# Retention heads: TensorE's order written out in the program instead of chosen by the scheduler, and a new order of the first head's loads

## The chip, the cores and the metric

The kernel runs on one core of one Trainium2 chip, as one program. The time is the device time of one execution in microseconds. A core has five engines that each work through a list of instructions in order: TensorE (PE in the profile; its weight loads are listed apart as PEld), VectorE (DVE), ScalarE (ACT), GpSimd (POOL) and SyncE (SP), which issues most of the DMAs. An instruction that needs another engine's result waits on a semaphore, and all that stands behind it in its list waits with it. Matmuls write to PSUM, in banks of 128 x 512 floats; VectorE and ScalarE take the results from there.

## The reference

Two layers of a decoder: a gated short convolution, then retention; behind each a SwiGLU feed-forward part (width 2816), RMS norms between. The width is 1024, with 512 prompt tokens and 32 sample tokens (8 sequences of 4), so 544 tokens. Retention has 4 heads with keys of 256 and values of 512. Cut to the part that the change touches:

```python
def retention_chunkwise(q, k, v, s0):              # chunks of 128 tokens
    def step(S, qkv):
        qc, kc, vc = qkv
        scores = jnp.einsum('bhid,bhjd->bhij', qc, kc) * decay
        inner = jnp.einsum('bhij,bhjv->bhiv', scores, vc)
        cross = jnp.einsum('bhid,bhdv->bhiv', qc, S) * cross_w[:, :, None]
        S_new = S * chunk_decay[:, None, None] + jnp.einsum('bhjd,bhjv->bhdv', kc * state_w[:, :, None], vc)
        return S_new, inner + cross
    ...
def retention_mixer(x, s0, pos, w_in, gn_g, w_out):
    z = x @ w_in
    q, k, v, g = jnp.split(z, [QK_DIM, 2 * QK_DIM, 2 * QK_DIM + V_DIM], axis=-1)
    ...
    q = rotary(q, pos)
    k = rotary(k, pos) * (HEAD_DK ** -0.5)
    o, S = retention_chunkwise(q, k, v, s0)
    ...                                             # each head's o: minus its mean, over its deviation
    out = (jax.nn.silu(g) * of) @ w_out
    return out, S
```

The sample sequences bring states of their own (8 x 4 heads x 256 x 512 floats, 16.8 MB), which are read, used and written back updated. Outputs are the tokens after the last norm, the convolution's buffers and the retention states.

## The kernel before

**Number format.** All products are of float32 precision by three products of rounded parts: each operand is split into a rounded part `h` (ACT, line 188) and a rest `l` (DVE, line 189); `mm3` (lines 163 to 165) and `project` (line 175) issue `h*h`, `h*l` and `l*h`. Every weight tile of 512 KB is thus loaded by SP, copied by ACT and subtracted by DVE before TensorE can use it (`load_piece`). With `adding=True` the subtraction is left to a DMA of GpSimd's queue that adds while it writes (line 196).

**Stages.** Convolution to about 159 us, the first feed-forward part to 575, then retention, and from 1083 on the second feed-forward part. The retention's part ahead of the heads stands in `ahead`: k, q and v of head 0 (to 631), then as jobs the gates of heads 0 to 2. The results go to memory and are loaded again (`qk_made`, `v_made`, `gate_made`). The four heads follow, in a loop (line 1299 on), at about 695, 812, 914 and 1016 us.

**A head.** While head h's sample operands are made, TensorE computes v of head h+1 in `value_products`: 8 k tiles, each 4 token tiles by 3 products of 128x512 (lines 816 to 818), and twice 4 small products for the sample tokens (line 824). The weights of v come in four pieces of two k tiles. Between them stand small steps: `keys` (transposes of the rotated keys, whose split parts are `knh` and `knl`), `sample_scores` (line 1211, result `s2`), `value_sample` (`v2`), `sample_operands` (`vs`, `kns`). Then:

- `state(c)`, for two halves of the prompt: 12 products into two banks (lines 163 to 165). After the first half the bank is split into `mid` (ACT, DVE), and the second half goes on in the same bank.
- `sample_outputs(i)` and `states_update(i)`, for four quarters of the sample states: four products with the state S (line 1237), four outer products (line 1253), and two updates `S = gamma * S + product` by DVE (line 1258, 128x1024 each); S is loaded in 1 MB and stored again. Three buffers hold S.
- `scores(c)`: 12 products of 128x256, masked by DVE into `sf` and split into `sh` and `sl`.
- `inner(i)`, for four token tiles: products with `mid` and of `sh`, `sl` with v. `normalized` takes mean and deviation with DVE (lines 1164, 1165, 222), GpSimd (line 223) and DVE again (line 1168, result `yn`).
- `gated_pair`, `gated`: four transposes of a `yn` (line 1192) and a product with the gate by DVE (line 1195).
- the next head's k and q: four `qk_project` of 48 products each (line 175), followed by DVE's rotation (lines 1011 to 1016).
- `out_project`: `yh` and `yl` from the gated values, 192 products by `project`.

The last head has no next v, k and q: its own gates are computed there instead (`gate_project`, four times 48 products).

**What sets the order.** The program is a list of operations in the order of the Python code; a scheduler places each on its engine by planned times, so that an engine's list can differ from the order of the code. `tc.issue_after(x)` keeps an operation behind another. Before, the heads are left to the scheduler with some such marks. Buffers are tiles with tags: two tiles of one tag share memory, and the later one waits for the last use of the earlier one. PSUM comes by `bank()` (single, `sm` in the profile) and `psum()` (a pair, `mm`).

Of the kernel before, what the change touches and what calls it, by code (L numbers as in the profile page):

```python
# [21 lines left out]
NH = 4  # L22
# [26 lines left out]
def hybrid_decode_kernel(ctx: ExitStack, tc: tile.TileContext, a: dict, o: dict):  # L49
# [211 lines left out]
    def drain(steps):  # L261
        for _ in steps:
            pass

# [532 lines left out]
    def value_products(h, xs, first=None, then=None, ws=None, sw=None):  # L797
# [3 lines left out]
        if ws is None:  # L801
            raw = []
            ws = [value_piece(h, c, raw, first is None, sw=None if c else sw) for c in range(2)]
        else:
            ws, raw = ws
        after = first() if first is not None else None
        for c in range(4):
            wh, wl = ws[c]
            if c < 2:
                ws.append(value_piece(h, c + 2, raw, first is None and c == 0, after=after if c == 0 else None))  # L810
            for k2 in range(2):
                kt = 2 * c + k2
                cw = slice(k2 * DV, (k2 + 1) * DV)
                for tt in range(4):
                    ts_, out = slice(tt * P, (tt + 1) * P), pv[tt]
                    nc.tensor.matmul(out, xh[kt][:, ts_], wh[:, cw], start=(kt == 0), stop=False)  # L816
                    nc.tensor.matmul(out, xh[kt][:, ts_], wl[:, cw], start=False, stop=False)  # L817
                    last = nc.tensor.matmul(out, xl[kt][:, ts_], wh[:, cw], start=False, stop=(kt == KT - 1))  # L818
            if c in (1, 2):
# [9 lines left out]
            if then is not None:  # L829
                then(c)  # L830
# [16 lines left out]
    def ahead(tp, fp, sw, one):  # L847
# [10 lines left out]
        qw, qpt = load_piece(a["rtqk"][0, 0], KT * P, adding=True), [bank(), bank()]  # L858
        project(qpt, *qw, 0, xh, xl, weave=steps)
# [11 lines left out]
        off(0, 0, qpt)  # L871
        xs = fp.tile([P, KT, NS], F32, tag="f", name=nm("xs"))
# [5 lines left out]
        pv, pvs = value_products(0, xs, then=operand_of, sw=sw)  # L878
# [43 lines left out]
    with ExitStack() as c2:  # L922
# [64 lines left out]
        def qk_project(h, st, which, dt, inside=None):  # L987
# [3 lines left out]
            if inside:  # L991
                project(pt, wh, wl, 0, xh, xl, last=False, ks=range(KP))
                inside()
                project(pt, wh, wl, 0, xh, xl, first=False, ks=range(KP, KT))
            else:
                project(pt, wh, wl, 0, xh, xl)
# [28 lines left out]
        def value_loaded(h, st):  # L1025
# [3 lines left out]
            nc.sync.dma_start(vw, v_made[h][:, 0:4, :])  # L1029
            st["loaded"] = nc.sync.dma_start(vsw, v_made[h][:, 4, :])  # L1030
# [9 lines left out]
        def value_sample(h, st):  # L1040

            pt = psum()
            v4 = tp.tile([P, 2, DV], F32R, tag="rot1", name=nm("v4"), bufs=1)
            split(v4[:, 0, :], v4[:, 1, :], st["v"][2])
            for i in range(2):
                nc.tensor.matmul(pt[:NS, 0, :], sum4, v4[:, i, :], start=(i == 0), stop=(i == 1))
            v2 = [tp.tile([NS, DV], F32R, tag=f"rt{i}", name=nm("v2"), bufs=1) for i in range(2)]
            split(*v2, pt[:NS, 0, :])
            st["v"][2] = v2

        def operands_made(h, st):

            qk_split(h, st, 1)
            qk_split(h, st, 0)
            sample_scores(h, st)
# [6 lines left out]
            keys(h, st)  # L1062

        def keys(h, st):
# [10 lines left out]
            split(knh, knl, pt)  # L1075
            pt = psum()
# [4 lines left out]
            st["kn"] = (knh, knl, k2)  # L1081
# [37 lines left out]
        def gate_project(h, st, n, inside=None, ws=None):  # L1119
# [3 lines left out]
            pt = [bank(), bank()] if inside else psum()  # L1123
            if inside:
                project(pt, wh, wl, 0, xh, xl, last=False, ks=range(KP))
                inside()
                project(pt, wh, wl, 0, xh, xl, first=False, ks=range(KP, KT))
            else:
                project(pt, wh, wl, 0, xh, xl)
            g = halves(st["gate"][:, n, :])  # L1130

            def scaled(p, gi, r):
                st["scaled"] = nc.vector.tensor_mul(gi, p, r)
# [25 lines left out]
        def normalized(src, tag="yn"):  # L1159
# [7 lines left out]
            yn = tp.tile([P, DV], F32, tag=tag, name=nm("yn"), bufs=2 if tag == "yn" else 1)  # L1167
# [38 lines left out]
        def sample_scores(h, st):  # L1206
# [10 lines left out]
            split(s2[:, 0, :], s2[:, 1, :], ss)  # L1217
            placed(pt[:, 1, :NS], s2[:, 0, :], s2[:, 1, :], 1)
# [42 lines left out]
        def out_project(h, st, rest=None):  # L1261
# [10 lines left out]
            split_gated(slice(0, HT if rest else T))  # L1272
            wide("mms")
            for n2 in range(4):
                wh, wl = load_piece(a["rtout"][h, n2], 2 * 4 * P)
                pts = []
                for n in range(2):
                    pts.append(psum())
                    if n2 == 0 and rest:
                        rest[n]()  # L1280
                        project(pts[n], wh, wl, n * 4 * P, yh, yl, hfs=(0,))
                    else:
                        project(pts[n], wh, wl, n * 4 * P, yh, yl)
                        residual(2 * n2 + n, pts[n])
                if n2 == 0 and rest:
                    split_gated(slice(HT, T))
                    for n in range(2):
                        project(pts[n], wh, wl, n * 4 * P, yh, yl, hfs=(1,))
                        residual(n, pts[n])
            wide("m")  # L1290

        def first_outputs(h, st):
            sample_outputs(h, st, 0)
            states_update(h, st, 0)
            states_load(h, st, 3)

        st = qk_start(0)
        qk_loaded(st)
        for h in range(NH):
            more = h + 1 < NH  # L1300
            st["S"] = {}

            def first():
                value_loaded(h, st)
                return st["loaded"] if h == 0 else None

            def then(c):
                if c == 0:
                    with tc.issue_after(last_load[0].ins) if h == 0 else ExitStack():
                        for i in range(2):  # L1310
                            states_load(h, st, i)
                elif c == 1:
                    states_load(h, st, 2)
                    operands_made(h, st)
                elif c == 2:
                    value_sample(h, st)

            if more:
                pv, pvs = value_products(h + 1, xs, first, then, None if h else next_v)
                va = tp.tile([P, 2, DV], F32, tag="rot1", name=nm("va"), bufs=1)  # L1320
                vb = [tp.tile([P, DV], F32, tag="yn", name=nm("vb")) for _ in range(2)]
                sample_operands(h, st)
# [4 lines left out]
                state(h, st, 0)  # L1327
                first_outputs(h, st)
                state(h, st, 1)
            else:  # L1330
                gw = load_piece(a["rtg"][h, 0], KT * P)
                first()
                for i in range(2):
                    states_load(h, st, i)
                gate_project(h, st, 0, lambda: operands_made(h, st), gw)
                value_sample(h, st)
                states_load(h, st, 2)
                sample_operands(h, st)
                state(h, st, 0)
                first_outputs(h, st)  # L1340
                gate_project(h, st, 1)
                state(h, st, 1)
            for c in range(2):
                scores(h, st, c)
            yn0 = normalized(inner(h, st, 0))
            sample_outputs(h, st, 1)
            yn1 = normalized(inner(h, st, 1))
            states_update(h, st, 1)
            sample_outputs(h, st, 2)
            p2 = inner(h, st, 2)  # L1350
            if more:
                nxt = qk_start(h + 1)
                for which in (1, 0):
                    qk_scale(nxt, which)
                with tc.issue_after(last_product[0].ins):
                    qk_project(h + 1, nxt, 1, 0)
                with tc.issue_after(last_product[0].ins):
                    gated_pair(h, st, (yn0, 0), (yn1, 1))
                sample_outputs(h, st, 3)
                p3 = inner(h, st, 3)  # L1360
                yn2 = normalized(p2)
                yns = normalized(st["po"])
                states_update(h, st, 2)

                def inside():
                    states_update(h, st, 3)
                    gated(h, st, yn2, 2)

                qk_project(h + 1, nxt, 1, 1, inside)
                yn3 = normalized(p3)  # L1370
                gated_pair(h, st, (yns, 4), (yn3, 3))
                qk_project(h + 1, nxt, 0, 0)
                qk_project(h + 1, nxt, 0, 1)
                out_project(h, st)
            else:
                yn2 = normalized(p2, "gt")
                gate_project(h, st, 2, lambda: states_update(h, st, 2))

                def inside():
                    sample_outputs(h, st, 3)  # L1380
                    states_update(h, st, 3)

                gate_project(h, st, 3, inside)
                with tc.issue_after(st["scaled"].ins):
                    yns = normalized(st["po"], "rot1")
                gated_pair(h, st, (yn0, 0), (yn1, 1))
                gated(h, st, yn2, 2)
                p3 = inner(h, st, 3)
                gated(h, st, yns, 4)
# [124 lines left out]
```

## Time and profile before

| | us |
|---|---|
| three runs | 1478.06, 1478.22, 1479.28 (median 1478.22) |
| profiled execution, its own time | 1478.13 |
| its span (first to last instruction) | 1475.8 |
| TensorE busy | 1458.5 (99%) |
| VectorE busy | 959.6 (65%) |
| ScalarE busy | 610.5 (41%) |
| GpSimd busy | 90.1 (6%) |
| mean granted clock of TensorE | 0.995 |

Times in the profile are in us from the span's start. A group is given as line, engine, operation, tile written <- tiles read. "Idle before" is the time that an engine stood still right before an instruction, with what released it. A group called `wh` or `w` may belong to any weight.

### The profile page before, as it was taken

To read this page: it belongs to the slowest core of one execution; us is meant where nothing else is said; L and a number is where in the kernel's file an instruction comes from. 1 tells how busy PE (TensorE), PEld (TensorE's weight loads), DVE (VectorE), ACT (ScalarE), POOL (GpSimd) and SP (SyncE) were. 2 spreads that over 40 slices of the span, in tenths; PEclk is the share of its full clock that TensorE was granted. 3 is DMA by queue.
4 is the path that set the end of the run, shared out by engine and by line. 5 is a ranking of instruction groups with operands and counts; after the bars stand their busy time and mean duration, and the time that the engine had idled before them with its cause. 6 is when DMAs were issued, how large, how long until landed. Compare 5 with 4: busy or idle time off the path is not lost.

```text
span 1475.8 us, 26100 instructions
## 1 busy us (share of the span) xinstructions
PE 1458.5 (99%) x10944; PEld 1382.9 (94%) x10944; DVE 959.6 (65%) x1470; ACT 610.5 (41%) x882; POOL 90.1 (6%) x112
## 2 busy tenths in 40 slices
PE   9999999999999999999899999999999999999998
PEld 9999999999999999799589698798799999999997
DVE  6645439847748546776686484595759857748645
ACT  5222355625425335466412322323265625525424
POOL 0100220000000003000000000000030000000002
PEclk9999999999999999999999999999999999999999
DMA  6222274232222334554784573672454232322322
GB/s 225 86 87 86 89 177 109 96 105 87 93 93 100 98 90 132 140 169 149 274 287 140 197 257 115 210 248 102 157 146 112 94 107 86 99 93 96 101 65 83
DMA packets 77445, 194.86 MB, mean 132 GB/s; under 512 B 7168, under 2 KB 24448, under 8 KB 76944
## 3 DMA queue, kind: packets, MB, share of 16 engines
q1 hardware_dynamic: 70272, 172.83, 34.6%
q0 software_dynamic: 2912, 10.56, 4.1%
q10 hardware_dynamic: 4144, 9.81, 1.7%
q8 instruction: 86, 1.41, 0.4%
q14 instruction: 31, 0.25, 0.1%
HBM read 162.29 MB, written 30.88 MB: 131 GB/s over the span
## 4 chain that ended last, share of the span: by engine, by line
PE 94%; DVE 3%; DMA 1%; issue 1%; ACT 1%; POOL 0%; DVEq 0%; POOLq 0%; ACTq 0%; SPq 0%
PE mm L175 35%; PE sm L461 30%; PE sm L175 15%; PE sm L817 2%; PE sm L818 2%; PE sm L163 2%; PE sm L816 2%; PE sm L1237 1%; PE sm L164 1%; PE sm L165 1%; DVE wl L189 1%; DMA wl<-in_rtqk_dram 1%; PE mm L1253 0%; DVE xl L201 0%; PE mm L1192 0%
## 5 line engine op out<-in xcount | busy, mean ns | idle before, releaser
L188 ACT ACTIVATE wh<-w 128x1024 fp32r<-128x1024 f32 (+4 forms) x210 | 204.5, 977 | 382.8 <-PE mm L175 185.7
L189 DVE TENSOR_TENSOR wl<-w,wh 128x1024 fp32r<-128x1024 f32 (+4 forms) x210 | 236.9, 1131 | 42.5 <-ACT wh L188 40.4
L461 PE MATMUL sm<-oh,wh 128*128 128x272 f32 x672 | 194.5, 289 | 0.0
L461 PE MATMUL sm<-oh,wl 128*128 128x272 f32 x672 | 194.2, 289 | 0.0
L461 PE MATMUL sm<-ol,wh 128*128 128x272 f32 x672 | 194.0, 289 | 0.0
L175 PE MATMUL mm<-xh,wh 128*128 128x272 f32 x804 | 170.1, 292 | 0.2
L175 PE MATMUL mm<-xh,wl 128*128 128x272 f32 x804 | 167.0, 290 | 2.4 <-DMA wl<-in_rtqk_dram 2.4
L175 PE MATMUL mm<-xl,wh 128*128 128x272 f32 x804 | 166.8, 289 | 0.0
L269 DVE TENSOR_TENSOR x<-x,mm 128x544 f32<-128x544 f32 x85 | 61.3, 721 | 144.3 <-PE mm L175 144.1
L461 PE MATMUL sm<-oh,l 128*128 128x272 f32 x504 | 145.6, 289 | 0.0
L461 PE MATMUL sm<-ol,h 128*128 128x272 f32 x504 | 145.4, 289 | 0.0
L461 PE MATMUL sm<-oh,h 128*128 128x272 f32 x504 | 145.3, 289 | 0.0
L175 PEld LDWEIGHTS mm<-xh,wl 128*128 128x128 f32 x804 | 126.1, 190 | 3.2 <-DMA wl<-in_rtqk_dram 2.6
L175 PEld LDWEIGHTS mm<-xh,wh 128*128 128x128 f32 x804 | 126.7, 190 | 1.7 <-ACT wh L188 0.5
L461 PEld LDWEIGHTS sm<-oh,wh 128*128 128x128 f32 x672 | 126.8, 189 | 1.1 <-ACT u L518 0.6
L175 PEld LDWEIGHTS mm<-xl,wh 128*128 128x128 f32 x804 | 127.0, 190 | 0.1
L461 PEld LDWEIGHTS sm<-oh,wl 128*128 128x128 f32 x672 | 126.8, 189 | 0.0
L461 PEld LDWEIGHTS sm<-ol,wh 128*128 128x128 f32 x672 | 126.6, 188 | 0.0
L189 DVE TENSOR_TENSOR l<-w,h 128x1024 fp32r<-128x1024 f32 x84 | 80.3, 956 | 56.3 <-ACT h L188 56.0
L175 PE MATMUL sm<-xh,wh 128*128 128x272 f32 x476 | 101.6, 291 | 0.0
L175 PE MATMUL sm<-xh,wl 128*128 128x272 f32 x476 | 99.8, 288 | 0.0
L175 PE MATMUL sm<-xl,wh 128*128 128x272 f32 x476 | 99.5, 287 | 0.0
(290 smaller groups left out, 3049.4 us busy)
## 6 DMA issues: line engine op xcount, KB each, us to landing
w<-in_ffgu_dram SPq DMA_DIRECT2D x88, 512.0 KB, 3.5
w<-in_ffdn_dram SPq DMA_DIRECT2D x96, 192.0 KB, 2.5
S<-in_rets_dram SPq DMA_DIRECT2D x16, 1024.0 KB, 7.1
out_rets_dram<-S SPq DMA_DIRECT2D x16, 1024.0 KB, 4.6
w<-in_cvin_dram SPq DMA_DIRECT2D x21, 512.0 KB, 3.4
w<-in_rtv_dram SPq DMA_DIRECT2D x16, 512.0 KB, 3.7
w<-in_rtqk_dram SPq DMA_DIRECT2D x16, 512.0 KB, 4.3
w<-in_rtg_dram SPq DMA_DIRECT2D x16, 512.0 KB, 3.8
```

The source lines that it names most:

```text
L163: nc.tensor.matmul(out, lh, rh, start=start, stop=False, skip_group_check=True)
L164: nc.tensor.matmul(out, lh, rl, start=False, stop=False, skip_group_check=True)
L165: last_product[0] = nc.tensor.matmul(out, ll, rh, start=False, stop=stop, skip_group_check=True)
L175: last_product[0] = nc.tensor.matmul(half(pt, hf)[:, :HT], w[:, c], act[k][:, hf * HT : (hf + 1) * HT], start=(first and k == ks[0] and i ...
L188: h = nc.scalar.activation(dh, src, AF.Copy)
L189: nc.vector.tensor_sub(dl, src, dh.bitcast(F32))
L269: last_residual[0] = nc.vector.tensor_add(xk, xk, p)
L461: nc.tensor.matmul(out, w[:, c], b[k][:, at, :], start=(first and k == 0 and i == 0), stop=(k == n - 1 and i == 2), skip_group_check=True,)
L816: nc.tensor.matmul(out, xh[kt][:, ts_], wh[:, cw], start=(kt == 0), stop=False)
L817: nc.tensor.matmul(out, xh[kt][:, ts_], wl[:, cw], start=False, stop=False)
L818: last = nc.tensor.matmul(out, xl[kt][:, ts_], wh[:, cw], start=False, stop=(kt == KT - 1))
L1237: last_product[0] = nc.tensor.matmul(st["po"][32 * g : 32 * g + 8, :], qm[:, dt, g, r, :], st["S"][i][:, g, :], start=False, stop=(i == 3) ...
```

## The change

1. All four heads move into a function `heads`, which runs with TensorE's order fixed: TensorE's list is the order of the code. The other engines' lists are still the scheduler's. `issue_after` marks and the `inside` arguments that the fixed order makes needless go.
2. Small steps are placed by k tile: `value_products` and `project` call a generator (`weave`) behind each k tile, and `behind(fns)` runs the function that is given for that tile. In head 0 the steps stand behind tiles 3 to 7, in heads 1 and 2 behind 0, 1, 2, 4, 5, 7.
3. Steps are cut: the keys of the samples get a step of their own (`keys_sample`), `sample_scores` and its placement are two, `value_sample` splits before it sums, q's scaling for the samples is `sample_queries`.
4. A quarter's outputs and update come together (`outputs(i)`). In heads 1 and 2 `outputs(0)` stands before the second `state`, and `outputs(1)` behind it; in head 0 both halves of the state come first. The order in the tail: scores, `outputs(2)`, three inner tiles, the fourth, `outputs(3)`, then k and q of the next head with gated transposes behind their fifth k tile.
5. `out_project` of the last head has its first two tiles cut at token 256 instead of 272, into single banks.
6. Ahead of the heads, q's second half is loaded and projected before v instead of after it; the third piece of the second head's v is loaded before head 0's v is fetched back (`vw`), and states 0 and 1 after `vw`.

```diff
+    def behind(fns):
+        for i in range(KT):
+            if i in fns:
+                fns[i]()
+            yield
...
-            ws, raw = ws
-        after = first() if first is not None else None
+            ws, raw, after = ws
+            ws.append(value_piece(h, 2, raw, after=after))
+        if first is not None:
+            first()
...
+                if k2 == 0:
+                    next(weave, None)
...
-            if then is not None:
-                then(c)
+            next(weave, None)
...
-        qw, qpt = load_piece(a["rtqk"][0, 0], KT * P, adding=True), [bank(), bank()]
-        project(qpt, *qw, 0, xh, xl, weave=steps)
+        qs = [load_piece(a["rtqk"][0, dt], KT * P, adding=True) for dt in range(2)]
+        qpt = [bank(), bank()]
+        project(qpt, *qs[0], 0, xh, xl, weave=steps)
...
+        qpt = psum()
+        project(qpt, *qs[1], 0, xh, xl)
+        off(0, 1, qpt)
...
-        qw = load_piece(a["rtqk"][0, 1], KT * P, adding=True)
         value_out(0, pv, pvs, list(zip(rows, outs)))
-        qpt = psum()
-        project(qpt, *qw, 0, xh, xl)
-        off(0, 1, qpt)
...
-                last = nc.sync.dma_start(t, src)
+                next_v[2:] = [nc.sync.dma_start(t, src)]
...
+            cut = 2 * P
+            split_gated(slice(0, cut if rest else T))
...
+                if n2 == 0 and rest:
+                    pts = [[bank(), bank()] for _ in range(2)]
+                    for i, c in enumerate((slice(0, cut), slice(cut, T))):
+                        if i:
+                            rest()
+                            split_gated(c)
+                        for n in range(2):
+                            project_part(pts[n][i], wh, wl, n * 4 * P, c)
...
+            sample = [
+                lambda: keys(h, st), lambda: keys_sample(h, st), lambda: sample_scores(h, st), scores_placed,
+                lambda: st["sums"](), lambda: sample_operands(h, st),
+            ]
             if more:
+                where = (3, 4, 5, 6, 7) if h == 0 else (0, 1, 2, 4, 5, 7)
+                fns = dict(zip(where, sample))
...
+                pv, pvs = value_products(h + 1, xs, splits, behind(fns), None if h else next_v)
+                load(2)
...
+            def outputs(i):
+                sample_outputs(h, st, i)
+                states_update(h, st, i)
...
+            state(h, st, 0)
+            if h == 0:
+                sample[5]()
+                state(h, st, 1)
+            outputs(0)
+            load(3)
+            gate(1)
+            if h:
+                state(h, st, 1)
+                outputs(1)
+            scores(h, st, 0)
+            if h == 0:
+                outputs(1)
+            scores(h, st, 1)
+            gate(2)
+            outputs(2)
+            yn0 = normalized(inner(h, st, 0))
+            yn1 = normalized(inner(h, st, 1))
+            gate(3)
+            yn2 = tp.tile([P, DV], F32, tag="rt1", name=nm("yn2"), bufs=1)
+            normalized(inner(h, st, 2), yn2)
+            if not more:
+                outputs(3)
+            p3 = inner(h, st, 3)
...
             if more:
+                normalized(p3, yn3)
+                outputs(3)
+                normalized(st["po"], yns)
                 nxt = qk_start(h + 1)
                 for which in (1, 0):
                     qk_scale(nxt, which)
+                qk_project(h + 1, nxt, 1, 0, {4: lambda: gated_pair(h, st, (yn0, 0), (yn1, 1))})
+                qk_project(h + 1, nxt, 1, 1, {4: lambda: gated_pair(h, st, (yn2, 2), (yn3, 3))})
+                qk_project(h + 1, nxt, 0, 0, {4: lambda: gated(h, st, yns, 4)})
                 qk_project(h + 1, nxt, 0, 1)
                 out_project(h, st)
+                return nxt
+            normalized(st["po"], yns)
+            gated_pair(h, st, (yn0, 0), (yn1, 1))
+            normalized(p3, yn3)
+            gated(h, st, yn2, 2)
+            gated(h, st, yns, 4)
+            out_project(h, st, lambda: gated(h, st, yn3, 3))
+
+        with tc.manual_schedule(engines={nc.tensor.engine}):
+            heads()
```

Line numbers shift: in the changed kernel S's update is line 1265, its products 1260, the gated transposes still 1195 (before 1192), yn 1171 and v's products 825 to 827.

More of the change, by code (lines that the diff above doesn't have):

```diff
@@ L1075, in keys, with keys_sample @@
             split(knh, knl, pt)
+            st["kn"] = [knh, knl, None]
+        def keys_sample(h, st):
+            krot = st["rot"][1]
             pt = psum()
@@ L1301, in hybrid_decode_kernel, with heads, head, load @@
+                for n in range(2):
+                    pt = psum()
+                    project(pt, wh, wl, n * 4 * P, yh, yl)
+                    residual(2 * n2 + n, pt)
+            wide("m")
+        def heads():
+            st = qk_start(0)
+            qk_loaded(st)
+            for h in range(NH):
+                st = head(h, st, h + 1 < NH)
+        def head(h, st, more):
             st["S"] = {}
-            def first():
+            def load(*which):
+                for i in which:
+                    states_load(h, st, i)
+            def splits():
@@ L1304, in first @@
                 value_loaded(h, st)
[L1305 to L1316, printed above, removed]
```

171 lines of the change are left out of this document (60 added, 111 removed).

## The prediction

> **What bounds the kernel now.** I read four views: the table of busy time, the chain of work that ended last, TensorE's waits, and the timeline around each wait, then the instruction list of every engine in the two programs with what each instruction waits for.
>
> ```profile
> PE 1458.5 (99%) x10944; PEld 1382.9 (94%) x10944; DVE 959.6 (65%) x1470; ACT 610.5 (41%) x882; POOL 90.1 (6%) x112
> ...
> PE 94%; DVE 3%; DMA 1%; issue 1%; ACT 1%; POOL 0%; DVEq 0%; POOLq 0%; ACTq 0%; SPq 0%
> ```
>
> TensorE (PE) is busy for 99% and carries 94% of the chain: whatever makes it wait lengthens the kernel, and all its waits together are some 10 us. That is also about the most that a new order can win.
>
> ```profile
> PE mm L175 <- DMA wl<-in_rtqk_dram: 2.4, 1, 2.4
> PE sm L816 <- ACT wh L188: 2.3, 1, 2.3
> PE sm L817 <- DVE wl L189: 2.0, 1, 2.0
> PE sm L301 <- DVE expo L102: 1.1, 1, 1.1
> PE sm L1192 <- DVE yn L1168: 0.6, 1, 0.6
> PE mm L1211 <- DVE rot L1015: 0.5, 1, 0.5
> PE mm L175 <- ACT yh L188: 0.5, 1, 0.5
> PE mm L1211 <- DVE rot L1016: 0.3, 1, 0.3
> ```
>
> The columns are total, times, longest. The first is in the work ahead of the heads (q's second half waits for its accumulating load); the second, third, sixth and eighth are in the first head's v products; L1192 and its neighbours are in the last head. Heads 1 and 2 (812 to 1016 us) show no wait of TensorE at all. Windows show what two of the waits leave behind:
>
> ```profile
> 624.80:628.20 3.40, 3.40 (x18) 3.40 (x17) 1.02 (x2) 2.73 (x4) 0.00 (x0) 0.50 0.80 243
> ...
> 709.00:717.00 8.00, 5.29 (x16) 3.85 (x17) 8.00 (x14) 2.34 (x3) 0.00 (x0) 0.57 1.01 366
> 812.00:914.00 102.00, 102.00 (x666) 84.89 (x665) 66.06 (x103) 28.30 (x38) 3.56 (x5) 1.00 0.56 192
> ```
>
> The column after the five engines is the granted clock: half speed for 3.4 us after the 2.42 us idle, and again after the idles at 706 to 713.
>
> ```profile
> 836.30 0.51 PE L1253 MATMUL mm<-vs,kns 32*128 32x512 f32 x4
> 836.73 0.38 PE L163 MATMUL sm<-qkh,qkh 128*128 128x256 f32 x1
> 836.84 1.22 DVE L1258 SCALAR_TENSOR_TENSOR S<-S,mm 128x1024 f32<-128x1024 f32 x1 [3.11 <-PE mm L1253]
> ...
> 837.98 1.28 DVE L189 TENSOR_TENSOR mid<-sm,mid 128x512 fp32r<-128x512 f32 x2
> ...
> 839.17 1.21 DVE L1258 SCALAR_TENSOR_TENSOR S<-S,mm 128x1024 f32<-128x1024 f32 x1
> 839.31 0.50 PE L163 MATMUL sm<-vh,knh 128*128 128x512 f32 x1
> ```
>
> Here lies the price of the change. In head 1 the state's second step (839.31) needs the vector engine's (DVE) `mid` split, which stands behind an S update that starts only after the L1253 products. TensorE doesn't notice: from 836.73 on it has scores to do.
>
> **The change part by part.** All TensorE instructions stay, as many in both programs; their order changes, and on the other engines the order that follows from it.
>
> *Removed.* (a) q's second half is projected before v instead of after it, and its accumulating load is issued where v's second was (588.5, landing by 594.5, wanted at 596.2): the 2.42 us go, and 3.4 us at half clock, in which 128x272 products followed each other by 0.227 us instead of 0.125, worth 3.4 x (1 - 0.125/0.227) = 1.5. Together 3.9. On SyncE's (SP) and GpSimd's queues v's pieces now follow q's second; they are also wanted 6 us later, so that the swap costs them nothing as long as q's products (48 x 0.125) stand before them. (b) The first head's third v piece is loaded ahead of `vw` (about 684 instead of 701.0), and the sample scores come later: idles of 2.25, 0.49, 0.25 and 1.96, and about 1.4 of half clock, 6.3 in all. (c) TensorE's changes of tile shape fall from 125 to 92; by the intervals of 0.326 beside 0.233 each costs 0.093, so 3.1. (d) In the last head idles of 0.63, 0.46 and 0.17: 1.3. Sum 14.6.
>
> *Added ahead of the heads.* (e) The gates now begin right after v; before, 6 us of q products (48 x 0.125) lay between. Their first weights' buffers are freed by v's own sample products, so load (3.5 us by the DMA rows), copy (1.04) and split (1.22) come out about 2 us after TensorE wants them. Bounds 0 (all of it covered by the copies of v) and 4 (the load queues as the accumulating one did, 8.3 instead of 5). I take 2.0.
>
> *Added in head 0's v products.* (f) The transposes of keys_sample wait for the `knl` split, and that stands in DVE's queue behind all of q's rotation. From the rows: DVE starts the L980 product of q at 702.6 (1.28), then the v split moved ahead (1.2), six rotation steps at 0.64, two `vl` and two `qkl` splits at 1.2, four `qm` at 0.1, `knl` 1.2, so about 715.0. TensorE has by then done four k tiles to 705.4, the sample products (0.9), eight transposes (0.9) and one tile more (12 x 0.233 = 2.8): 710.0. Stall 5.0. Behind it wait nothing but TensorE's own products, and ACT's copies of `wh`, which have slack.
>
> *Added in the heads' tails.* The rows give DVE's prices: S update 1.14 from start to start, mid split 0.64, statistics 0.69 with 0.17 and 0.15 behind, GpSimd's power 0.5, yn 0.80, gate product 0.68; some 0.25 passes from an engine's end to its reader's start.
>
> (g) Heads 1 and 2, state 1: outputs(0) now directly precedes it, and DVE's list has both S updates before the mid split. From TensorE's first L1265 product: 0.54 to DVE's start (836.30 to 836.84), 1.14, 1.14, 0.64, 0.1: 3.56, less the 0.45 that the four products take: 3.1. The cover of before, twelve score products, comes after.
>
> (h) Inner 3 takes the bank that yn0 frees. Inner 0 to 2 take 18 products, 4.2 us. DVE has two S updates of step 2 and one `sl` split first (2.85), then three statistics (2.1), small steps and GpSimd (0.5), yn0 (0.8): 6.2. Stall 2.0.
>
> (i) The k projection of the next head waits for S3's first update, which stands behind p3's statistics, po's statistics and yn3: 4.1 after inner 3, of which step 3's products cover 1.6. Stall 2.6.
>
> (j) Two pairs of gated transposes, each pair through one bank: the second four wait for the gate product, 0.75 each: 1.5.
>
> Per head 3.1 + 2.0 + 2.6 + 1.5 = 9.2, for two heads 18.4. In head 0 the state steps stand together before outputs, so (g) is the mid split behind ACT's copies alone, 1.9; with 1.9, 2.7 (S3's load may add up to 1.5) and 1.5 it makes 8.0.
>
> (k) The last head by the same walk: `v2` is made and placed without anything between (ACT and DVE behind gate work) 1.7; gate 1 for S0 1.2; the second gated pair behind S3's second update, statistics and a gate product 1.8; the out-projection's first part, for `yh` and `yl` behind two gate products and yn3, 2.5; its second part, for the last gate product and split, 1.5. Sum 8.7. Gates 2 and 3 cover the other S updates.
>
> (l) Half clock. Seven new idles are of 2.5 us or longer: 5.0 and 2.7 in head 0, 3.1 and 2.6 in heads 1 and 2, 2.5 in the last. Nearest rows: both idles over 2.2 us brought it, at 1.4 to 1.5, that of 0.63 did not. Bounds: only the 5.0 (1.5) and all seven (10.3). With two rows to go by I take the middle, 5.9.
>
> [...]
>
> Sum: 2.0 + 5.0 + 18.4 + 8.0 + 8.7 + 5.9 = 48.0 added, 14.6 removed, +33.4. The profiled execution took 1478.13 us (span 1475.8 and 2.3 around it), the median of three is 1478.22. Forecast 1511.
>
> **The rivals.** *R1, the clock stays.* The same stalls without half clock but for one: +29, 1507; with all seven, +38, 1516. These lie around the forecast. [...] *R2, half of the stalls.* Every wait was priced from TensorE running at its full pace up to it; where one stall lets DVE catch up, the next may shrink, as (h) after (g), and (j) after (i). If the tails of heads 0 to 3 (35.1) cost half: 1478.1 + 33.4 - 17.5 - 3 (fewer half clocks) = 1491. Against it: DVE is idle before the S updates (3.11 in the row above), so (g) has no backlog to lose. *R3, faster.* DVE runs the mid splits and yn as soon as their inputs stand, so that no S update lies in front of them, and TensorE meets only the waits through one bank (3 x 1.5 in (j), 2 in the last head) and 2 in (f): 1478.1 - 14.6 + 8.5 = 1472. It turns the sign once the added waits fall below 14.6, a third of mine. For it: DVE is busy for 65% only. Against it: engines take their lists in order, and the lists have the S updates in front. *R4, nothing changes*: the removed and added waits cancel within 3 us. It would take additions of 12 to 18 us, between R2 and R3.
>
> **How the numbers follow.** Forecast with R1 0.66, R2 0.21, R3 0.11, R4 0.02. A measurement of this kernel can tell about 0.2%, 3 us, from no change. Slower than that: 0.87, same 0.02, faster 0.11. The range leaves out R3 and R4 and the far ends of (e) and (l): from 1488 (R2 and somewhat less) to 1522 (all half clocks, 4 in (e), S3's load late).
>
> **What would show it.** Right, if TensorE's waits of after list `mid` for L163 twice at about 3 us, `yn` for L163 three times at 2, S for L175 three times at 2.6, `knl` for L1085 once near 5, and the DMA wait at `wl<-in_rtqk_dram` is gone; and if heads 1 and 2 take 110 us instead of 102. Wrong, if L163 waits for no `mid` (g), if the first gates begin later than 2 us after v (e), or if the granted clock stays at 1.00 in heads 1 and 2 (l). The prediction fails altogether if those two heads still take 102 us.

## The result, and the profile after

The changed kernel takes 1510.36 us (median of five runs, 1510.05 to 1514.75) where the kernel before takes 1478.06 (median of five): a ratio of 1.0228, with a 95% interval of 1.0211 to 1.0244. 1511 was forecast. The profiled execution took 1510.09 us, with a span of 1507.7. Busy time and the chain of work, from the page of the changed kernel:

```profile
PE 1457.8 (97%) x10944; PEld 1383.8 (92%) x10944; DVE 962.8 (64%) x1470; ACT 611.8 (41%) x882; POOL 87.8 (6%) x112
...
PE 89%; DVE 5%; DMA 2%; issue 1%; ACT 1%; POOL 1%; SPq 0%; DVEq 0%; POOLq 0%; ACTq 0%
```

TensorE (PE) does the same work in the same busy time, but only 89% of the chain is its own now, after 94%; VectorE's (DVE) share went from 3 to 5. TensorE's waits (total, times, longest) name the places:

```profile
PE mm L175 <- DVE S L1265: 8.5, 4, 2.5
PE sm L163 <- DVE mid L189: 7.8, 3, 3.0
PE mm L1195 <- DVE gate L1198: 6.2, 7, 1.5
PE sm L163 <- DVE rs L222: 5.0, 3, 1.7
PE mm L1085 <- DVE knl L189: 4.3, 1, 4.3
PE sm L468 <- DVE wl L189: 3.6, 2, 2.4
PE sm L164 <- DVE yl L189: 1.8, 1, 1.8
PE sm L163 <- ACT yh L188: 1.6, 2, 1.3
...
PE mm L964 <- DVE v L189: 0.7, 1, 0.7
PE mm L963 <- ACT v L188: 0.7, 1, 0.7
```

Seven of the eight largest have a VectorE instruction as their releaser. Before, all TensorE waits together were 9.5 us; now they are 42.0 (both are the sum of its idle times over the span). The wait for `wl<-in_rtqk_dram` is gone, as are those in head 0's v products, but for the new one at L1085. The same stretch of head 1 as before, from the changed kernel's timeline:

```profile
841.29 0.51 PE L1260 MATMUL mm<-vs,kns 32*128 32x512 f32 x4
841.83 2.35 DVE L1265 SCALAR_TENSOR_TENSOR S<-S,mm 128x1024 f32<-128x1024 f32 x2 [3.08 <-PE mm L1260]
844.09 1.28 DVE L189 TENSOR_TENSOR mid<-sm,mid 128x512 fp32r<-128x512 f32 x2
...
844.83 0.80 PE L163 MATMUL sm<-vh,knh 128*128 128x512 f32 x1 [3.04 <-DVE mid L189]
845.43 0.63 PE L164 MATMUL sm<-vl,knh 128*128 128x512 f32 x1
845.85 0.63 PE L165 MATMUL sm<-vh,knl 128*128 128x512 f32 x1
```

VectorE waited 3.08 us for the products of S0, then made both updates, and only then split `mid`, for which TensorE stood still for 3.04 us. The products behind it take 0.63 us instead of 0.39 and follow each other by 0.42 instead of 0.23: half clock. The windows say the same (the column after the five engines is the granted clock):

```profile
812.00:914.00 102.00, 93.22 (x591) 76.00 (x590) 60.61 (x95) 24.58 (x34) 2.71 (x5) 0.97 0.53 188
845.00:850.80 5.80, 5.80 (x16) 3.75 (x20) 1.51 (x2) 1.04 (x2) 0.00 (x0) 0.50 0.71 243
957.20:963.40 6.20, 5.75 (x16) 3.92 (x20) 2.12 (x3) 0.82 (x2) 0.00 (x0) 0.50 0.66 224
```

From the products of S0 in head 1 to those in head 2 it is 112.8 us (841.29 to 954.10); before, a head took 102.

Further on in head 1, the wait at inner 3:

```profile
858.30 1.21 DVE L1265 SCALAR_TENSOR_TENSOR S<-S,mm 128x1024 f32<-128x1024 f32 x1
861.71 0.81 DVE L1171 TENSOR_SCALAR yn<-sm,mv,rs 128x512 f32<-128x512 f32 x1
862.57 0.50 PE L163 MATMUL sm<-mid,qkh 128*128 128x512 f32 x1 [1.73 <-DVE rs L222]
```

VectorE's second update of S2 ends at 859.51, the statistics and `yn` of inner 0 follow, and 0.05 us after the end of `yn` (862.52) TensorE goes on in the bank that it frees. The profile puts such waits down to the small instruction for `rs` that runs at the same moment; in the run with `scores(0)` moved, below, two of the three stand as `yn`.

Put together, the span grew by 31.9 us. TensorE's idle time grew by 32.5. The time that half clock adds (each interval of two products in such a stretch, less the mean interval of the same two shapes elsewhere) went from 3.5 to 8.6, so +5.1. All other intervals fell by 4.0, with the changes of tile shape. That makes 33.6; 1.7 are within what the means of rare pairs of shapes leave open.

### The profile page after: what moved, and what is told of

Its sections match the earlier page's. It is cut to its first block, busy times and chain, and to the rows that moved or that the text cites. A ratio compares the mean times of both kernels' runs of the same rounds, so it can differ in the third digit from the quotient of the medians.

```text
span 1507.7 us, 26084 instructions
## 1 busy us (share of the span) xinstructions
PE 1457.8 (97%) x10944; PEld 1383.8 (92%) x10944; DVE 962.8 (64%) x1470; ACT 611.8 (41%) x882; POOL 87.8 (6%) x112
## 4 chain that ended last, share of the span: by engine, by line
PE 89%; DVE 5%; DMA 2%; issue 1%; ACT 1%; POOL 1%; SPq 0%; DVEq 0%; POOLq 0%; ACTq 0%
PE mm L175 35%; PE sm L468 29%; PE sm L175 14%; PE sm L825 2%; PE sm L826 2%; PE sm L827 2%; DVE S L1265 1%; DMA S<-in_rets_dram 1%; PE sm L163 1%; PE sm L164 1%; PE sm L165 1%; DMA w<-in_rtg_dram 1%; DVE wl L189 1%; PE sm L1244 1%; PE mm L835 0%
## 5 line engine op out<-in xcount | busy, mean ns | idle before, releaser
L175 PE MATMUL mm<-xh,wh 128*128 128x272 f32 x836 | 175.4, 291 | 9.6 <-DVE S L1265 8.5
L175 PE MATMUL mm<-xh,wl 128*128 128x272 f32 x836 | 173.0, 289 | 0.0
L175 PE MATMUL mm<-xl,wh 128*128 128x272 f32 x836 | 172.2, 287 | 0.0
L175 PEld LDWEIGHTS mm<-xh,wh 128*128 128x128 f32 x836 | 130.2, 188 | 11.8 <-DVE S L1265 9.7
L175 PEld LDWEIGHTS mm<-xl,wh 128*128 128x128 f32 x836 | 130.9, 188 | 0.1
L175 PEld LDWEIGHTS mm<-xh,wl 128*128 128x128 f32 x836 | 130.3, 188 | 0.6 <-DVE wl L189 0.2
L175 PE MATMUL mm<-xh,f 128*128 128x272 f32 x576 | 99.3, 288 | 0.0
L468 PEld LDWEIGHTS sm<-oh,h 128*128 128x128 f32 x504 | 94.9, 188 | 0.2 <-ACT h L188 0.2
L468 PEld LDWEIGHTS sm<-ol,h 128*128 128x128 f32 x504 | 95.0, 188 | 0.0
```

The lines of the kernel that those rows point to most:

```text
L175: last_product[0] = nc.tensor.matmul(half(pt, hf)[:, :HT], w[:, c], act[k][:, hf * HT : (hf + 1) * HT], start=(first and k == ks[0] and i ...
L468: nc.tensor.matmul(out, w[:, c], b[k][:, at, :], start=(first and k == 0 and i == 0), stop=(k == n - 1 and i == 2), skip_group_check=True,)
```

## The experiments

Each starts from the changed kernel. "Idle" is the sum of TensorE's idle times in the run's profile and "half clock" the time that it adds, as above; for the changed kernel 42.0 and 8.6, for the kernel before 9.5 and 3.5. Each ratio is to the kernel before on the same chip. "Less" and "more" are differences of the medians to the changed kernel's 1510.36 us. The kernel before took 1478.06 us beside the changed kernel and 1478.26 to 1479.13 beside the experiments, and an interval of a ratio reaches some 0.1 to 0.2% (1.5 to 3 us) to each side, so that differences under some 4 us are not clear of the noise. Where theories lie closer than that, the waits decide, and they are those of one execution of each run.

**The mid splits first.** Only VectorE's queue changes:

```diff
+                    st["mid_split"] = last_rest[0]          # VectorE's part of the split, in state(c = 0)
...
-            outputs(0)
+            with tc.issue_after(st["mid_split"].ins) if h in (1, 2) else ExitStack():
+                outputs(0)
```

> The changed kernel, but in heads 1 and 2 VectorE's two updates of S0 are queued behind the two mid splits; TensorE's order is untouched. Theory A (each wait of the tails stands alone on the path, and what it costs includes the half clock behind it): the two waits of 3.04 us for mid go, and with them both stretches at half clock of 6.83 us, which cost 2.9 and 2.8: 11.8 us less, 1498.5. Theory B (VectorE's work is the limit of a tail, so a removed wait comes back at the next one): the S1 updates and yn0 come later by what is won, less than 4 us in all. Theory C (the clock falls whatever the cause, TensorE's low load in the tails being enough): 6.1 us less, half clock stays, 1504.3.

Measured: 1501.98 us, ratio 1.0155 (1.0140 to 1.0170), 8.4 less. Idle 35.9: both waits of 3.04 are gone and no other changed by more than 0.25 us. From its timeline:

```profile
839.73 1.47 DVE L189 TENSOR_TENSOR mid<-sm,mid 128x512 fp32r<-128x512 f32 x2 [1.29 <-ACT mid L188]
...
840.99 0.51 PE L1263 MATMUL mm<-vs,kns 32*128 32x512 f32 x4
...
841.42 0.50 PE L163 MATMUL sm<-vh,knh 128*128 128x512 f32 x1
...
841.52 2.35 DVE L1268 SCALAR_TENSOR_TENSOR S<-S,mm 128x1024 f32<-128x1024 f32 x2 [0.32 <-PE mm L1263]
```

The split now uses the time in which VectorE stood idle, and S's updates run under the state's second step. So the cause is VectorE's order, not its load, and theory A holds for the idle time. The half clock behind these waits went too, but in this execution it came behind the waits for S in both heads (at 864 and 973 us), which had kept full clock before; its sum only fell from 8.6 to 7.2, and the execution's mean granted clock is 0.993, that of the changed kernel's 0.992. In the two profiles that makes 7.6 us less, and not 11.8. The time alone can't tell: by the ratios it is 10.8 less.

**Half of the cover back.** `scores(h, st, 0)` moved between `outputs(0)` and the second `state` in heads 1 and 2:

> The changed kernel, but in heads 1 and 2 scores(0), twelve products of 0.12 us, stand between outputs(0) and the second state step, so that the wait for mid is shortened by 1.44 us to 1.6 and not removed. Theory A with a fixed grid (in both traces all half-clock stretches begin on one grid of 3.413 us, and only where more than about half of the window before was idle): 1.6 us idle of 3.41 brings no half clock: 2 x (1.44 + 2.85) = 8.6 us less, 1501.8. Theory C (half clock after any wait of TensorE in this place): 2.9 us less, 1507.5. Theory B: less than 2 us.

Measured: 1504.91 us, ratio 1.0172 (1.0155 to 1.0189), 5.5 less. The two waits are 1.41 us and no half clock follows them, as theory A has it. Idle fell to 38.3. The half clock's sum stayed at 8.7, since this execution, the slowest of the four (1507.12 us, mean granted clock 0.992, that of the others 0.993 to 0.994), had it behind the gates, three steps of it in head 0, and behind the wait for S in head 1 instead. The expected 8.6 forgot that the other waits draw anew.

**S3's update later.**

```diff
-                outputs(3)
+                sample_outputs(h, st, 3)
...
-                qk_project(h + 1, nxt, 1, 1, {4: lambda: gated_pair(h, st, (yn2, 2), (yn3, 3))})
+                qk_project(h + 1, nxt, 1, 1, {0: lambda: states_update(h, st, 3), 4: lambda: gated_pair(h, st, (yn2, 2), (yn3, 3))})
```

> The changed kernel, but in heads 0 to 2 the update of S3 stands behind the first k tile of the second k projection (which has banks of its own) instead of ahead of the first. Theory A: the waits of 2.26, 2.45 and 2.46 us at the first k product go, 7.2 us less, 1503.2, no half clock being at stake there. Theory B: S3's update then stands in VectorE's queue ahead of the second gated pair and of the rotation, whose readers wait: less than 3 us, with new waits for S at L1195.

Measured: 1502.61 us, ratio 1.0160 (1.0144 to 1.0175), 7.8 less. Idle 34.9, lower by 7.2: theory A.

**S2's update later.** `outputs(2)` ahead of inner 0 becomes `sample_outputs(h, st, 2)` there and `states_update(h, st, 2)` behind inner 1:

> The changed kernel, but in heads 0 to 2 the update of S2 (products and VectorE's two instructions) stands behind inner 1 instead of ahead of inner 0. Theory A: the statistics and yn0 no longer queue behind S2's updates; TensorE's idle time falls by the three waits of 1.50, 1.73 and 1.73 us at inner 3, from 42.0 to 37.0 us in the profile, and the time by about 5, give or take half clock. Theory B (VectorE's backlog comes back at S3): the waits at the first k product grow by as much as inner 3 wins, idle time stays within 2 us of 42.0.

Measured: 1512.09 us, ratio 1.0222 (1.0204 to 1.0240): no gain. Idle fell to 37.2 as theory A has it: the three waits at inner 3 are gone, and head 0 got one of 0.78 for S's load. But half clock rose from 8.6 to 17.5. Nine stretches of it lie in this execution, before TensorE's last work, among them one behind each wait for S at the next k products (2.83, 2.16 and 2.15 us). It is not this execution alone: the mean granted clock of the run's four executions is 0.985 to 0.988, that of the changed kernel's five 0.988 to 0.992. The profile shows what happened; the time alone would have said that S2's place doesn't matter.

**Pairs turned in one go.**

```diff
             for i, (yn, it) in enumerate(pair):
+                turned(yn, pt[:, i, :])              # four transposes
+            for i, (yn, it) in enumerate(pair):
                 gated(h, st, yn, it, pt[:, i, :])    # only the gate product now
```

> The changed kernel, but a gated pair turns both of its tiles (eight transposes) before the first of its two gate products, instead of turning, multiplying, turning, multiplying in one pair of banks. Theory A: the six waits of 0.78 us go (4.7) and the one of 1.49 in the last head shrinks by about 0.7; idle time falls from 42.0 to 36.6 us. Theory B: the transposes wait for something else at the same moment (yn1 or yn3), and idle time falls by less than 2 us.

Measured: 1505.93 us, ratio 1.0189 (1.0172 to 1.0205), 4.4 less; idle 37.3. The six waits of 0.78 are gone. That of the last head stayed at 1.55, as it waits for `yn` now and not for the gate product.

**q's second half behind v again**, with its accumulating load, and then with VectorE's subtraction (`adding=True` left out in that load):

> The changed kernel, but q's second half stands behind v again, loaded there, as in the kernel before. Theory A (the two places cost nearly the same): the waits of 1.16 and 2.43 us at the first gates go (3.6), the wait for the accumulating load comes back (2.4) and, by the place of the idle time on the clock's grid, half clock with it (0 or 1.5): between 1.2 less and 0.3 more. By the prediction's terms (3.9 won, 2.0 lost) it would be 1.9 more.

> As the run with q's second half behind v, but its rest part is made by VectorE's subtraction instead of GpSimd's accumulating transfer, which took 8.3 us to land. Theory A: VectorE has the time for one more instruction of 1.22 us there, so that neither the wait for the load nor those at the gates remain: idle time falls by 3.6, from 42.0 to 38.4. Theory B: VectorE is full at this place (7.75 of 10 us busy from 610 to 620 in the kernel before) and the operands of the gates come later instead: idle time within 1.5 us of 42.0.

Measured: 1512.80 us (ratio 1.0235, 1.0216 to 1.0253), idle 39.8 and half clock 11.9; and 1509.55 us (1.0211, 1.0194 to 1.0227), idle 39.1. In the first the 3.6 us at the gates went and 2.1 came back at `wl<-in_rtqk_dram`, with half clock behind it (623 to 626 us); with 2.2 us less idle and 3.3 more of half clock it is no faster than the changed kernel. The time lies 2.4 above it, beyond both expectations but not clear of the noise (1.0 by the ratios). Moving q thus saves little by itself: the wait passes from one load to the next. In the second both are gone but for 0.6 at the gates.

**keys_sample later in TensorE's order** (`where = (3, 6, 7)` in head 0, the last two steps behind the v products):

> The changed kernel, but in head 0 keys_sample stands behind k tile 6 instead of 4, the sample scores behind 7 and the two steps after them behind the v products. Theory A: TensorE reaches keys_sample 5.6 us later, when knl is split; the wait of 4.28 us and the half clock behind it (1.4) go: 5.7 us less, 1504.7. Theory B: the later steps wait in its place (v2 and its placement as in the last head, 1.4; mid behind them), 2 to 4 us less.

Measured: 1515.20 us, ratio 1.0244 (1.0229 to 1.0260): 4.8 more, by the ratios 2.4, so that a loss isn't shown, but theory A's gain is excluded. Idle is 41.7, as before the edit. The wait for `knl` and head 0's for `mid` (1.76) are gone, and these stand in their place:

```profile
PE mm L1052 <- ACT v L188: 3.9, 1, 3.9
...
PE mm L963 <- ACT s L188: 1.1, 1, 1.1
...
PE sm L826 <- DVE wl L189: 0.8, 1, 0.8
...
PE mm L1052 <- DVE v L189: 0.7, 1, 0.7
```

The sums of the sample values (L1052), with nothing beside them now, wait for a copy that stands behind others in ScalarE's queue; half clock lasted from 726 to 736 us. Theory A failed, and theory B, with its 2 to 4 us less, was too mild.

**VectorE's order in head 0** (`knl` directly behind q's rotation, then the fourth v piece; the `vl` splits, q's split and `qm` queued behind v's sample split by `issue_after`):

> The changed kernel, TensorE's order untouched, but in head 0 VectorE's queue is changed: the knl split comes directly behind q's rotation, the fourth v piece behind it, and the vl splits, q's split and qm stand last. Theory A (the wait at keys_sample is a matter of VectorE's order): knl is ready about 710 instead of 714.4, the wait of 4.28 us goes and with it the half clock (1.4); small waits of up to 1 us each for the fourth piece, s2 and vl may come: idle time from 42.0 down to 37.7 to 40, time 3 to 6 us less. Theory B (VectorE is full from 697 to 715, so the order only says who waits): 4 us of waits come back at the fourth piece, at s2 and at vl, time within 2 us of 1510.

Measured: 1508.47 us (1506.36 to 1513.0), ratio 1.0210 (1.0191 to 1.0229). The 4.28 us are gone, and this execution has no half clock in head 0; 0.75 came at the fourth piece, `mid` rose from 1.76 to 2.37, and S's load cost 0.66. Idle 39.6, so 2.4 less and not 4.3. Both theories are half right: over half of the wait was VectorE's order, and the rest came back at other readers.

**All together**, and **with the last head's order free again** (its steps as in the kernel before, outside the fixed order):

```diff
         with tc.manual_schedule(engines={nc.tensor.engine}):
-            heads()
+            st = heads()            # heads 0 to 2
+        last_head(NH - 1, st)
```

> All edits that took idle time away, together: mid splits ahead of S0's updates in heads 1 and 2, S2's update behind inner 1, S3's update in the second k projection, pairs turned in one go, q's second half behind v with VectorE's subtraction, and VectorE's new order in head 0. Theory A (the waits add up one by one): idle time 42.0 - 6.2 - 4.4 - 7.2 - 4.7 - 2.9 - 3 = 13.6 us, half clock 2 to 5 us instead of 8.6, so 1475 to 1479: level with the kernel before. Theory B (the waits share VectorE's time, so that they can be removed singly but not together): idle time over 20 us, 1485 or more.

> As the run with all edits, and the last head as in the kernel before, its order left to the scheduler and its steps where they were, but for the cut of its out-projection at token 256. Theory A: the last head's waits (6.9 us of idle time, 1.5 to 3 of half clock) fall to the 1.3 us that they were: 7 to 8 us less than with all edits alone, 1468 to 1472, some 0.5% faster than the kernel before. Theory B: the last head's waits come from its shared banks and not from the order, so less than 3 us.

Measured: 1478.18 us, ratio 1.0001 (0.9993 to 1.0010), idle 15.7 and half clock 5.5; and 1472.41 us, ratio 0.9965 (0.9954 to 0.9976), idle 11.8 and half clock 1.6. The waits add up. The idle times that the single runs won sum to 28.1 us, and all of them together won 26.3. Freeing the last head won less than the 7 to 8 us that theory A had: its waits fell from 7.7 to 2.9 us and not to 1.3. What is left of TensorE's waits in the faster kernel, the largest:

```profile
PE sm L1260 <- DMA S<-in_rets_dram: 3.4, 1, 3.4
PE sm L163 <- DVE mid L189: 2.3, 1, 2.3
PE sm L163 <- ACT yh L188: 1.3, 1, 1.3
```

So with heads 0 to 2 in a fixed order a kernel 0.35% faster than the one before was to be had, once VectorE's queue was set with it and the last head was left to the scheduler. Heads 1 and 2 show no wait at all there.

It isn't faster for waiting less: TensorE stands idle for 11.8 us, against 9.5 in the kernel before. The two profiled spans, 1472.6 and 1475.8, differ by 3.2: 2.3 more idle, 1.9 less from half clock, and so 3.6 less in all other intervals. Which part of the change brings the gain is open: the earlier load of the third v piece, which with the later sample scores takes away 6.3 us by the prediction's count, was never run with the scheduler's order, and in the other intervals the tile shapes can't be told from the rest.

**S2's update early in head 0**, for the wait of 3.4 us:

> As the run with all edits and the last head free, but in head 0 S2's update stands ahead of inner 0 again. In the run before, S3 shares its buffer with S0, whose store and S3's load follow each other, and TensorE waited 3.4 us for S3's load there, with 1.6 us of half clock behind. Theory A (moving S2's update behind inner 1 pulled sample_outputs(3) nearer to S3's load, by 4 us or so): the wait for S falls below 1 us and yn0's wait of 1.5 us comes back, without half clock: 3 us less, 1469.5. Theory B (S3's load is late by itself, because its buffer comes free late): the wait for S stays, with yn0's wait on top of it or hidden in it: within 1.5 us of 1472.4.

Measured: 1473.22 us, ratio 0.9963 (0.9951 to 0.9975). The wait for S is gone and yn0's 1.5 us are back, as theory A had it; but now the wait for `mid` (2.37 us) brought half clock, from 728 to 735. No gain, and the 3 us of theory A are not shown.

## Why the prediction was right

The forecast of 1511 rests on terms that can be read off the trace one by one. Those added, predicted and measured in us:

| step | predicted | measured |
|---|---|---|
| (e) first gates | 2.0 | 3.6 (1.16 + 2.43) |
| (f) `knl` for keys_sample | 5.0 | 4.28 |
| (g) state 1, `mid`, heads 1 and 2; head 0 | 6.2; 1.9 | 6.1; 1.76 |
| (h) inner 3, yn0, heads 1 and 2; head 0 | 4.0; 1.9 | 3.5; 1.5 |
| (i) k projection, S3, heads 1 and 2; head 0 | 5.2; 2.7 | 4.9; 2.26 |
| (j) gated pairs | 4.5 | 4.7 |
| (k) last head | 8.7 | 7.6 |
| (l) half clock | 5.9 | 8.6 |
| sum | 48.0 | 48.7 |

That the sums lie within 1 us of each other is in part luck: (e) and (l) came out 4.3 us larger than forecast, the others together 3.6 smaller.

Of the removed ones, (a), (b) and (d) went as said, with 8.6 us of idle time and 3.5 of half clock; (c) is 3.1 against 4.0 for all intervals that are neither idle nor at half clock, in which the tile shapes can't be told from the rest.

- (g) to (j) were right in place and size. The experiments show the cause that the prediction named for (g) in heads 1 and 2, (h), (i) and (j): a reader behind VectorE's S updates, or transposes that must wait for a gate product. In (j) it is not one bank, though: a pair's tile is of two banks (`psum()`), each four transposes fill one, and the second four wait (0.78 us) although they write the other. For (g) in head 0 no run took the wait away alone. The measured waits of (g) to (i) are up to 0.45 us shorter than forecast; the 0.25 us that I put between an engine's end and its reader may be too much (0.05 in the view of inner 3 above).
- (e) was mis-sized: 3.6 for 2.0. It priced one late weight; there are two, the first (1.16 us, from 626.9) and a later one (2.43, from 634.6). Together they lie below the upper bound of 4. The move of q (a) won 3.9 and lost 3.6, and the run with q in its old place shows that the two nearly cancel.
- (f) was right as a wait. That VectorE's place in the queue was its whole cause is too strong: of 4.3 us, 1.9 come back elsewhere when the queue is changed, and moving TensorE's step instead gained nothing.
- (l) was mis-sized, and its mechanism was wrong in one point. I let the length of a wait decide, and of seven waits forecast at 2.5 us or more I took the middle between one and all. In the changed kernel four waits of 2.26 to 2.46 us had no half clock behind them, the two of 3.04 had 6.83 us of it each, twice as long as the 3.4 us that I had taken from the kernel before (where the second stretch, from 710.1, is 6.83 long as well), and in the last head two waits of 0.68 and 0.72 brought 3.4 us. So the length of a wait alone does not tell it; what the profiles show beside it stands below. The lower bound, half clock behind the 5.0 us stall alone, is not shown by any run: in the changed kernel it stands behind the 4.28 us that came in its place and at three more places.
- R1, the clock's two ends, bracketed the result. R2 (half of the stalls, since VectorE catches up in one stall for the next) is refuted by the adding up of single runs. R3 (VectorE meets its readers in time) is refuted by the waits. That the kernel with all edits and the last head free took 1472.4, where R3 had 1472, is a coincidence: TensorE's order, the last head and q's load were changed there too.
- One slip of the pen: the products of S are L1260 in the changed kernel, where (g) calls them L1265, which is the update. And three of its sums are a little off: (f)'s queue adds up to 715.3 and not 715.0, (i) to 2.5 and not 2.6, and the upper end of the range from its parts to 1519.4 (1511.5 + 4.4 + 2.0 + 1.5) and not 1522.

## What to carry to other kernels

When the order of one engine is fixed by hand, waits can move to the queues of the others, which the scheduler still fills: here VectorE's. Read those queues beside it: for every operation of the fixed engine, what stands ahead of its producer, and what the fixed engine does meanwhile. Durations from the old trace were enough to price the waits in the tails to half a microsecond each, before anything ran; the waits at the gates were off by 1.6, those in the last head by 1.1 in all.

A changed time under 0.5% (7 us here) says little about one wait when the time at half clock changes with it. Compare the sum of the idle times and the stretches at half clock as well: one edit here removed 5 us of waiting and gained nothing in time (S2's update later: idle 42.0 to 37.2 us, half clock 8.6 to 17.5).

## What the runs showed of the hardware

In the profile of the kernel before, the granted clock is at half from 624.77 us (for 3.41 us) and from 710.11 (6.83), in that of the changed kernel from 714.30 (3.41), 844.00 (6.83), 956.64 (6.83) and 1045.39 (3.41); one more stretch in each begins behind TensorE's last work (1471.28 and 1502.77). Within a profile the starts ahead of that lie whole multiples of 3.413 us apart, to within 0.01 of such a step: 25 in the one, 38, 71 and 97 from the first in the other. Counted from the start of the span, the first border of a step lies at 0.14 us in the one and at 0.91 in the other. In these profiles the idle time within a step goes far to tell the clock of the next. From the changed kernel, three pairs of steps:

```profile
751.84:755.26 3.42, 2.39 (x17) 0.71 (x15) 3.10 (x6) 0.00 (x0) 0.67 (x2) 1.00 0.80 307
755.26:758.67 3.41, 2.06 (x16) 2.06 (x17) 2.67 (x5) 0.00 (x0) 0.54 (x1) 1.00 0.01 4
840.59:844.00 3.41, 1.21 (x12) 0.19 (x4) 2.17 (x2) 1.14 (x2) 0.00 (x0) 1.00 0.46 175
844.00:847.42 3.42, 2.59 (x6) 2.10 (x7) 2.51 (x4) 0.00 (x0) 0.00 (x0) 0.50 0.68 253
1041.98:1045.39 3.41, 2.01 (x9) 0.96 (x8) 2.61 (x5) 2.98 (x5) 0.00 (x0) 1.00 0.04 6
1045.39:1048.80 3.41, 3.41 (x10) 2.60 (x9) 0.88 (x2) 0.60 (x2) 0.00 (x0) 0.50 0.47 148
```

The second column is TensorE's busy time. The wait of 2.26 us across a border (with the small gaps beside it, 1.03 and 1.35 us idle) had no half clock behind it; the step that holds 2.2 us of a wait of 3.04 did. From 600 to 1110 us of the two profiles, the five steps at full clock with 2.03 to 3.41 us idle were followed by half clock; so was one of the 16 with 1.03 to 1.67 us, and none of the 267 with less. That one is the third pair here, with 1.40 us, at the sample steps of the last head, and its busy time is mostly products of 32 rows or columns. Whether they have to do with it was not tested. "More than about half", as an expectation above reads the same two profiles, leaves this step out. In the run with S2's update later, a step with 2.41 us idle (756.13 to 759.54) was followed by half clock; in that with `scores(0)` moved, one with 0.69 (845.15 to 848.55) was not.

Of the nine steps at half clock in the same stretch of the two profiles, the three with 0.83, 1.01 and 2.70 us idle were followed by another, and the six with up to 0.51 were not. For the wait of 3.04 us in head 1 that makes two steps: 2.2 us of it lie in the step before 844.00, and the 0.83 us left in the step from there (second line of the second pair).

A wait of some 2 us thus cost about 1.5 us more (the one of 2.42 in the kernel before: 3.4 us with 128x272 products every 0.227 us instead of 0.125) or nothing (the four of 2.26 to 2.46 in the changed kernel). That fits the spread between executions of one kernel: the changed kernel's fastest, 1510.05 us, had a mean granted clock of 0.992, its slowest, 1514.75, one of 0.988.
